# Another order inside the unit of attention: value products three units late, additions last

## The chip, the cores and the metric

The kernel runs on one core of a Trainium2 chip. The metric is the time of one execution in microseconds (us), as the device measures it; the median of several runs is compared. The engines are named as in the profile: PE (matrix products), PEld (its weight loads), DVE (vector), ACT (scalar and activation), POOL (GpSimd) and SP (which issues most DMA transfers).

## The reference

One layer of a decoder trunk, sequence 2048, width 1024, 16 query heads of 64 columns in two key/value groups, all in float32. The part that matters here is sliding-window attention with a sink:

```python
logits = jnp.einsum('bnqhgd,bnkhd->bnhgqk', qb, kb) * (HEAD_DIM ** -0.5) + bias
logits = jnp.where(mask, logits, NEG_INF)          # window of 128, blocks of 128
probs = jax.nn.softmax(jnp.concatenate([logits, sink], axis=-1), axis=-1)[..., :-1]
out = jnp.einsum('bnhgqk,bnkhd->bnqhgd', probs, vb)
...
a = attention * jax.nn.silu(a_gate);  a = a @ w_attn_proj
p = (GroupLinear(MultiScaleCausalPool(p_in)) * pool_scale) * silu(p_gate);  p = p @ w_pool_proj
y = (sigmoid(m_a) * a + sigmoid(m_p) * p) @ w_out * (1 + gate)
x = layer_norm(alpha * x + y)
```

## The kernel before, in words

The sequence is worked in two passes (s = 0 and 1) of 1024 positions. Each pass has a phase of gate products and a phase of attention; a last phase, the mixing, has the output products and the layer norm. Products in float32 are made of three products of a high and a low part (`mm3`): the high part is a rounded copy made on ACT, the low part (`low`) is the difference made on DVE or POOL.

`attention` is one loop of 69 units, written out in Python. The first 64 units (`N`) are pairs of heads by blocks of 128 queries: `j = n // 8` is the pair of heads, `t` the half of the pass and `b` the block in it. Within each engine the order is that in which the loop writes the instructions (the wrappers `pe`, `act`, `dve`, `pool`, `sp` keep program order); engines wait for each other by semaphores that the framework sets from the tiles that are written and read. A tile of a tag with `bufs=1` can be written anew only when every reader of its predecessor is done.

One block of queries passes through the loop over several units. Before the change these are, for the block of unit n:

- unit n: four score products into a bank `lg` (`score_mms`); on DVE two fused additions of the bias with a running minimum ("maxima", `tensor_tensor_reduce`, shown as CUSTOM_DVE_ANT_0); on ACT two exponentials with their sums.
- unit n + 1: the reciprocal of the sums on DVE; the first head's probabilities are normalised on ACT, the second head's on DVE (`tensor_scalar`).
- unit n + 2: four transposes into the bank `pt` (`turn_mms`); a high part `pth` (ACT) and a low part `ptl` (DVE) of them; and at the end of the unit four value products into the bank `pv` (`value_mms`).
- unit n + 3: half of `pv` is copied to `o2` (ACT), and two additions on DVE put the sum of both halves into `o`.

So a unit of the loop writes work of four blocks. Beside it each unit has half of a projection of 24 products of 128x512 (`parts[i]`, twelve products in a unit), whose weights come from HBM. What the projection has made is taken up by further steps behind the unit's own work: `take_q` in units 6 and 0 of every eight (two ACT copies and two DVE instructions, for the queries of the next pair of heads), `pool_sums` and `pool_diff` for the pooling branch (POOL and DVE), `finish`, in which POOL multiplies `o` or the pooled values by their gates, and high and low parts of weights. The value bank `pv`, the bank `pt`, and the tiles `pth` and `ptl` have one buffer each; `lg` has two and `L` three:

```python
        return ps.tile([P, CH], F32, tag=tag, bufs={"mm": 4, "lg": 2, "pt": 1, "pv": 1}[tag], name=tag)
```

Of the kernel before, what the change touches and what calls it, by code (L numbers as in the profile page):

```python
# [12 lines left out]
F32 = mybir.dt.float32  # L13
F32R = mybir.dt.float32r
AF = mybir.ActivationFunctionType
ALU = mybir.AluOpType
# [3 lines left out]
P = 128  # L20
# [3 lines left out]
CH = 512  # L24
NCH = S // CH
NB = CH // P
HEADS = 16
HD = 64
# [31 lines left out]
def kernel(  # L60
# [70 lines left out]
    def low(engine, dst, src, hi):  # L131
        engine.tensor_tensor(dst, src, as32(hi), ALU.subtract)  # L132
# [617 lines left out]
    def attention(ph, s, q0, nxt):  # L750
# [4 lines left out]
        def ld(name, src):  # L755
            x = tp.tile([P, CH], F32, tag="ld", bufs=3, name=name)
            nc.sync.dma_start(x, src)
            return x
# [83 lines left out]
        def score_mms(j, b, q, qs):  # L842
            k0 = P if s == 0 and b == 0 else 0
            lg = bank("lg").rearrange("p (h k) -> p h k", h=2)
            for h in range(2):
                for hl in range(2):
                    mm(
                        lg[:, h, k0:],
                        qs[:, h, q * P : (q + 1) * P],
                        kk[:, j // 4, hl, b * P + k0 : (b + 2) * P],  # L850
                        start=hl == 0,
                        stop=hl == 1,
                    )
            return lg, k0

        def turn_mms(L, k0):
            pt = ps.tile([P, 2, 2, P], F32, tag="pt", bufs=1, name="pt")
            for hf in range(k0 // P, 2):
                for h in range(2):
                    pe.transpose(pt[:, hf, h, :], L[:, h, hf * P : (hf + 1) * P], ident)  # L860
            return pt
# [20 lines left out]
        bts = {0: bias_tile(0)}  # L882
        tiles = {0: fetch(*slots[0][:2])}
        parts, accs, sums = {}, {}, {}
        lgs, exps, Ls, pvs, outs, ags, pgs = {}, {}, {}, {}, {}, {}, {}
        opened = []
        act.activation(warm, mhalf, AF.Exp)

# [32 lines left out]
        for n in range(N + 5):  # L921
            j, t, b = n // U, n // NB % 2, n % NB
            if n < N:
                lgs[n] = score_mms(j, n % U, b, qs[j, t])
            pt = None
            if n - 2 in Ls:
                L, k0 = Ls.pop(n - 2)
                pt = turn_mms(L, k0)
            if n - 1 in exps:
                sm = exps[n - 1][2]  # L930
                dve.reciprocal(sm, sm)
            if n - 3 in pvs:
                pv = pvs.pop(n - 3)
                jj, tt, bb = (n - 3) // U, (n - 3) // NB % 2, (n - 3) % NB
                if bb == 0:
                    outs[jj, tt] = tp.tile([P, CH], F32, tag="o", bufs=2, name="o")
                if bb == 1:
                    ags[jj, tt] = ld("ag", gates_d["ag"][s, jj, tt])
                o2 = tp.tile([HD, 2, P], F32, tag="o2", bufs=2, name="o2")
                act.copy(o2, pv[HD:])  # L940
                for h in range(2):
                    dve.tensor_tensor(
                        outs[jj, tt][h * HD : (h + 1) * HD, bb * P : (bb + 1) * P], pv[0:HD, h, :], o2[:, h, :], ALU.add
                    )
            if n - 1 in exps:
                E, e0, sm = exps[n - 1]
                act.activation(E[:, 0, e0:256], E[:, 0, e0:256], AF.Copy, scale=sm[:, 0:1])
            if pt is not None:
                h0 = k0 // P
                pth = tp.tile([P, 2, 2, P], F32R, tag="pth", bufs=1, name="pth")  # L950
                ptl = tp.tile([P, 2, 2, P], F32R, tag="ptl", bufs=1, name="ptl")
                act.copy(pth[:, h0:], pt[:, h0:])
            if n < N:
                lg, c0 = lgs.pop(n)
                L = tp.tile([P, 2, 260], F32, tag="L", bufs=3, name="L")
                nm = tp.tile([P, 2], F32, tag="nm", bufs=4, name="nm")
                sm = tp.tile([P, 2], F32, tag="sm", bufs=4, name="sm")
                act.copy(L[:, :, 256], nsink[:, 2 * j : 2 * j + 2])
                for h in range(2):
                    dve.tensor_tensor_reduce(  # L960
                        L[:, h, c0:256],
                        lg[:, h, c0:],
                        bts[j][:, h, c0:],
                        1.0,
                        nsink[:, 2 * j + h : 2 * j + h + 1],
                        ALU.add,
                        ALU.min,
                        nm[:, h : h + 1],
                    )
                    act.activation(  # L970
                        L[:, h, c0:257],
                        L[:, h, c0:257],
                        AF.Exp,
                        bias=nm[:, h : h + 1],
                        scale=-1.0,
                        accum_out=sm[:, h : h + 1],
                    )
                exps[n] = (L, c0, sm)
            if pt is not None:
                low(dve, ptl[:, h0:], pt[:, h0:], pth[:, h0:])  # L980
            if n - 1 in exps:
                E, e0, sm = exps.pop(n - 1)
                dve.tensor_scalar(E[:, 1, e0:256], E[:, 1, e0:256], sm[:, 1:2], None, ALU.mult)
                Ls[n - 1] = (E, e0)
            i = n // 2
            if i < len(slots):
                kind, m, st = slots[i]
                if n % 2 == 0:
                    accs[kind, m, st], parts[i] = projection(us[st])
                parts[i](tiles[i // 2][1:], 4 * (n % 2), 4 * (n % 2) + 4)  # L990
            elif n >= 60:
                fill_one(n)
            if pt is not None:
                pvs[n - 2] = value_mms((n - 2) // U, (n - 2) % U, k0, pth, ptl)


            w = n // 4 + 1
            if n % 4 == 0 and 2 * w < len(slots):
                tiles[w] = fetch(*slots[2 * w][:2])
            if w in tiles and tiles[w][0] is not None:  # L1000
                raw, hi, lo = tiles[w]
                if n % 4 == 1:
                    act.copy(by_two(hi), raw)
                if n % 4 == 2:
                    low(pool, by_two(lo), raw, by_two(hi))
            if n % U == 2 and j + 1 < KT:
                bts[j + 1] = bias_tile(j + 1)
            for st in range(2):
                if n % U == 6 + 2 * st - (U if st else 0) and (m := j + 1 - st) < KT and ("q", m, st) in accs:
                    qs[m, st] = take_q(accs.pop(("q", m, st)))  # L1010
            for what in puts:
                put(pool if n >= 64 else sp, *what)
            puts.clear()
            for at, x, which in ((57, 0, 0), (60, 1, 0), (62, 0, 1), (64, 1, 1)):
                if n == at:
                    early_hi(x, which)
                if n == at + 1:
                    early_lo(x, which)
            if n in (59, 62):
                nxt_group[n // 62].mid()  # L1020
            if n == 64:
                opened[0].append(nxt_group[0].w[:, 0, :])
                act.copy(opened[0][4], opened[0][0])
            for st in range(2):
                if n % U == 3 + 2 * st and (j, st) in sums:
                    pgs[j, st] = ld("pg", gates_d["pg"][s, j, st])
                if n % U == ((4, 6 + (j + 1 < KT))[st]) and (j, st) in sums:
                    pl = pool_diff(j, sums.pop((j, st)), accs.pop(("mix", j, st)))
                    finish("p", pin_d[s], j, st, pl, pgs.pop((j, st)))
            for st in range(2):  # L1030
                if n % U == 2 + 2 * st and ("mix", j, st) in accs:
                    sums[j, st] = pool_sums(j, st, accs["mix", j, st])
            for x in [x for x in outs if n == x[0] * U + x[1] * NB + NB + 2]:
                finish("a", ain_d[s], *x, outs.pop(x), ags.pop(x))

            if n in (26, 42):
                fill_set("T1", n // 42, nxt_store["T1"], sp)
            for start, name in ((57, "B11"), (58, "B21"), (59, "T2"), (61, "B22")):
                if n == start:
                    for half in range(2):  # L1040
                        fill_set(name, half, nxt_store[name], sp)
            if n == 51:
                for q in nxt_group:
                    q.load(ph, False)
# [467 lines left out]
```

## Time and profile before

| | |
|---|---|
| median of 3 runs | 1761.59 us (1759.8 to 1762.62) |
| the profiled execution | 1766.1 us, span in the profile 1763.9 us |
| mean granted PE clock | 0.991 |
| busy: PE, PEld | 1702.4 us (97%), 1427.4 us (81%) |
| busy: DVE, ACT, POOL | 1206.9 us (68%), 934.1 us (53%), 794.2 us (45%) |
| the two passes of attention | about 417 to 690 us and 1018 to 1290 us of the span |

How to read the rows: the timeline has start and length in us, engine, line, operation, and `out<-in` by the names of the tiles, then the shapes; `x4` stands for so many instructions in a row, and in brackets stands how long the engine was idle before and what ended that. A row of a stretch has its length and then, for each engine, the busy time and the instructions, then the granted clock, the share of the DMA engines and GB/s. A row of waits has the total, the times and the longest. A row of a tile has the shortest, median and longest duration in ns. Nearly all instructions of the loop have the line of a wrapper, L56, so they are told apart by their tiles.

### The profile page before, as it was taken

How to read it: one execution, taken by the hardware profiler on the slowest of the kernel's cores; microseconds unless marked ns; L12 is line 12 of the kernel's file. 1: busy time of each engine (PE TensorE's matmuls, PEld its weight loads, DVE VectorE, ACT ScalarE, POOL GpSimd, SP SyncE). 2: the span in 40 equal slices, each digit the busy share in tenths (PEclk: the TensorE clock that was granted, in tenths of full speed). 3: DMA queues.
4: the chain of work that ended last, by engine and by line, in shares of the span. 5: the costliest groups of instructions: out<-in, count | busy, mean ns of one | idle time of the engine just before them, and what ended most of it. 6: DMA issues, size and time to landing. Idle time of an engine off the chain costs nothing. (4 is left out here: it accounts for less than half of the span.)

```text
span 1763.9 us, 24990 instructions
## 1 busy us (share of the span) xinstructions
PE 1702.4 (97%) x8248; PEld 1427.4 (81%) x8248; DVE 1206.9 (68%) x2178; ACT 934.1 (53%) x1973; POOL 794.2 (45%) x618
## 2 busy tenths in 40 slices
PE   6899999999999998999999999999999989999997
PEld 5688888878888887888788888888888867888785
DVE  5977665655777776766655367777867676764777
ACT  4644444545777775544444377777734343423452
POOL 2154444431356567534434125456763562364542
PEclk9999999999999999999999999999999999999998
DMA  9385767844354567787777634544796675789442
GB/s 364 117 289 174 269 208 270 273 145 132 108 174 147 171 217 288 249 288 253 258 264 261 232 96 135 177 159 141 265 349 215 197 256 169 240 302 386 162 143 108
DMA packets 180466, 381.30 MB, mean 216 GB/s; under 512 B 18785, under 2 KB 39281, under 8 KB 180337
## 3 DMA queue, kind: packets, MB, share of 16 engines
q1 hardware_dynamic: 173696, 363.92, 60.5%
q0 software_dynamic: 3552, 11.56, 1.7%
q10 hardware_dynamic: 3088, 4.23, 0.8%
q8 instruction: 65, 1.06, 0.3%
q14 instruction: 65, 0.52, 0.1%
HBM read 244.35 MB, written 138.44 MB: 217 GB/s over the span
## 5 line engine op out<-in xcount | busy, mean ns | idle before, releaser
L56 PE MATMUL mm<-set_B,w_set 128*128 128x512 f32 x3240 | 798.7, 395 | 14.5 <-ACT u L376 6.3
L56 PEld LDWEIGHTS mm<-set_B,w_set 128*128 128x128 f32 x3240 | 603.3, 189 | 142.6 <-DVE w_set L132 10.3
L56 PE MATMUL lg<-set_T,w_set 128*128 128x512 f32 x2088 | 509.1, 394 | 18.4 <-DVE w_set L132 11.0
L56 PEld LDWEIGHTS lg<-set_T,w_set 128*128 128x128 f32 x2088 | 391.4, 189 | 111.0 <-DVE w_set L132 17.9
L132 DVE TENSOR_TENSOR w_set<-W,w_set 128x1024 fp32r<-128x1024 f32 x162 | 227.9, 1407 | 185.8 <-ACT w_set L325 180.8
L325 ACT CAST w_set<-W 128x1024 fp32r<-128x1024 f32 x162 | 169.8, 1049 | 251.6 <-PE mm L56 190.3
L56 PE MATMUL mm<-set_T,w_set 128*128 128x512 f32 x1080 | 265.5, 394 | 0.0
L56 PEld LDWEIGHTS mm<-set_T,w_set 128*128 128x128 f32 x1080 | 200.5, 188 | 41.0
L294 POOL TENSOR_TENSOR W<-W,A 128x512 f32<-128x512 f32 x56 | 82.1, 1466 | 227.6 <-DMA W<-in_win_dram 63.6
L303 POOL TENSOR_TENSOR W<-W 128x512 f32<-128x512 f32 x56 | 80.5, 1438 | 174.5 <-DVE w_set L132 165.2
L56 DVE TENSOR_TENSOR o<-pv,o 64x128 f32<-64x128 f32 x256 | 72.3, 283 | 89.8 <-ACT o L56 86.9
L56 ACT ACTIVATE L<-L,nm 128x257 f32<-128x257 f32 (+1 forms) x256 | 127.1, 498 | 9.3 <-DVE nm L56 3.9
L298 POOL TENSOR_TENSOR W<-W 128x512 f32<-128x512 f32 x56 | 90.5, 1618 | 84.7 <-DVE w_set L132 75.6
L56 DVE CUSTOM_DVE_ANT_0 L<-lg,bt,nsink 128x256 f32<-128x256 f32 (+1 forms) x256 | 111.6, 473 | 5.0 <-PE lg L56 0.8
L299 POOL TENSOR_TENSOR W<-W 128x512 f32<-128x512 f32 x56 | 84.7, 1513 | 37.9 <-DMA W<-in_win_dram 21.9
L56 POOL TENSOR_TENSOR w_set<-W,w_set 128x1024 fp32r<-128x1024 f32 x14 | 33.7, 2404 | 139.6 <-ACT w_set L56 96.9
L56 POOL TENSOR_TENSOR p<-nxt,pg 128x512 f32<-128x512 f32 x32 | 41.7, 1302 | 105.5 <-DVE sm L56 101.8
L56 ACT COPY o<-pv 64x256 f32<-64x256 f32 x128 | 47.3, 370 | 78.0 <-PE pv L56 77.2
L56 DVE TENSOR_TENSOR ptl<-pt,pth 128x512 fp32r<-128x512 f32 (+1 forms) x128 | 85.7, 669 | 1.9 <-ACT pth L56 1.7
L56 PE MATMUL lg<-kk,qs 128*128 128x256 f32 (+1 forms) x512 | 80.5, 279 | 0.0
L56 ACT ACTIVATE L<-L,sm 128x256 f32<-128x256 f32 (+1 forms) x128 | 64.2, 502 | 29.8 <-DVE sm L56 29.8
L56 ACT CAST pth<-pt 128x512 fp32r<-128x512 f32 (+1 forms) x128 | 73.5, 574 | 10.3
(212 smaller groups left out, 2296.3 us busy)
## 6 DMA issues: line engine op xcount, KB each, us to landing
W<-in_win_dram SPq DMA_DIRECT2D x48, 512.0 KB, 5.5
w_set<-wmix_d SPq DMA_DIRECT2D x32, 512.0 KB, 5.4
W<-in_win_dram SPq DMA_DIRECT2D x34, 256.0 KB, 3.7
A<-in_win_dram SPq DMA_DIRECT2D x34, 256.0 KB, 5.1
ag_d<-sig SPq DMA_DIRECT2D x32, 256.0 KB, 3.8
pg_d<-sig SPq DMA_DIRECT2D x32, 256.0 KB, 4.0
ma_d<-sig SPq DMA_DIRECT2D x32, 256.0 KB, 4.0
mp_d<-sig SPq DMA_DIRECT2D x32, 256.0 KB, 4.0
```

The source lines that it names most:

```text
L56: return lambda *args, **kw: self.tc.keep_in_program_order(op(*args, **kw))
L132: engine.tensor_tensor(dst, src, as32(hi), ALU.subtract)
L294: e.tensor_tensor(self.w[:, 1, :], self.w[:, 2, :], self.a22, ALU.add)
L298: e.tensor_tensor(x[:, 1, :], x[:, 1, :], x[:, 0, :], ALU.subtract)
L299: e.tensor_tensor(x[:, 2, :], x[:, 0, :], x[:, 2, :], ALU.subtract)
L303: e.tensor_tensor(x[:, 3, :], x[:, 3, :], x[:, 1, :], ALU.subtract)
L325: a.copy(by_two(hi), raw)
```

## The change

The value products of a block move from the end of unit n + 2 to unit n + 3, behind the scores of that unit and ahead of its transposes. `pth` and `ptl` are kept for that in `turned`. The projection is written directly behind the transposes. On ACT the copy of the sinks and the first normalising come first, then the copies of `pv` and `pt`, then the exponentials. On DVE the order is: reciprocal, the two maxima, the low part, the second normalising, and at last the two additions (before: reciprocal, additions, maxima, low part, normalising). The load of the attention gate (`ld("ag")`) is issued with the additions.

```diff
-                lgs[n] = score_mms(j, n % U, b, qs[j, t])
-            pt = None
+                lg, c0 = score_mms(j, n % U, b, qs[j, t])
+            pt = pv = None
+            if n - 3 in turned:
+                pv = value_mms((n - 3) // U, (n - 3) % U, *turned.pop(n - 3))
             if n - 2 in Ls:
                 L, k0 = Ls.pop(n - 2)
-                pt = turn_mms(L, k0)
+                pt, h0 = turn_mms(L, k0), k0 // P
+            i = n // 2
+            if i < len(slots):
...
+                parts[i](tiles[i // 2][1:], 4 * (n % 2), 4 * (n % 2) + 4)
+            elif n >= 60:
+                fill_one(n)
+            if n < N:
...
+                act.copy(L[:, :, 256], nsink[:, 2 * j : 2 * j + 2])
             if n - 1 in exps:
-                sm = exps[n - 1][2]
-                dve.reciprocal(sm, sm)
-            if n - 3 in pvs:
...
+                E, e0, r = exps[n - 1]
+                dve.reciprocal(r, r)
+                act.activation(E[:, 0, e0:256], E[:, 0, e0:256], AF.Copy, scale=r[:, 0:1])
+            if pv is not None:
                 o2 = tp.tile([HD, 2, P], F32, tag="o2", bufs=2, name="o2")
                 act.copy(o2, pv[HD:])
-                for h in range(2):
-                    dve.tensor_tensor(
-                        outs[jj, tt][h * HD : (h + 1) * HD, bb * P : (bb + 1) * P], pv[0:HD, h, :], o2[:, h, :], ALU.add
-                    )
...
             if pt is not None:
                 low(dve, ptl[:, h0:], pt[:, h0:], pth[:, h0:])
+                turned[n - 2] = k0, pth, ptl
             if n - 1 in exps:
-                E, e0, sm = exps.pop(n - 1)
-                dve.tensor_scalar(E[:, 1, e0:256], E[:, 1, e0:256], sm[:, 1:2], None, ALU.mult)
+                E, e0, r = exps.pop(n - 1)
+                dve.tensor_scalar(E[:, 1, e0:256], E[:, 1, e0:256], r[:, 1:2], None, ALU.mult)
                 Ls[n - 1] = (E, e0)
...
-            if pt is not None:
-                pvs[n - 2] = value_mms((n - 2) // U, (n - 2) % U, k0, pth, ptl)
+            if pv is not None:
+                jj, tt, bb = (n - 3) // U, (n - 3) // NB % 2, (n - 3) % NB
+                if bb == 0:
+                    outs[jj, tt] = tp.tile([P, CH], F32, tag="o", bufs=2, name="o")
+                if bb == 1:
+                    ags[jj, tt] = ld("ag", gates_d["ag"][s, jj, tt])
+                for h in range(2):
+                    dve.tensor_tensor(
+                        outs[jj, tt][h * HD : (h + 1) * HD, bb * P : (bb + 1) * P], pv[0:HD, h, :], o2[:, h, :], ALU.add
+                    )
```

More of the change, by code (lines that the diff above doesn't have):

```diff
@@ L884, in attention @@
         parts, accs, sums = {}, {}, {}
-        lgs, exps, Ls, pvs, outs, ags, pgs = {}, {}, {}, {}, {}, {}, {}
+        exps, Ls, turned, outs, ags, pgs = {}, {}, {}, {}, {}, {}
         opened = []
@@ L932, in attention @@
-            if n - 3 in pvs:
[L933 to L938, printed above, removed]
+                pt, h0 = turn_mms(L, k0), k0 // P
+            i = n // 2
+            if i < len(slots):
+                kind, m, st = slots[i]
+                if n % 2 == 0:
+                    accs[kind, m, st], parts[i] = projection(us[st])
+                parts[i](tiles[i // 2][1:], 4 * (n % 2), 4 * (n % 2) + 4)
+            elif n >= 60:
+                fill_one(n)
@@ new lines, in attention @@
+            if n < N:
+                L = tp.tile([P, 2, 260], F32, tag="L", bufs=3, name="L")
+                nm = tp.tile([P, 2], F32, tag="nm", bufs=4, name="nm")
+                sm = tp.tile([P, 2], F32, tag="sm", bufs=4, name="sm")
+                act.copy(L[:, :, 256], nsink[:, 2 * j : 2 * j + 2])
+            if n - 1 in exps:
+                E, e0, r = exps[n - 1]
+                dve.reciprocal(r, r)
+                act.activation(E[:, 0, e0:256], E[:, 0, e0:256], AF.Copy, scale=r[:, 0:1])
@@ L939, in attention @@
+            if pv is not None:
                 o2 = tp.tile([HD, 2, P], F32, tag="o2", bufs=2, name="o2")
                 act.copy(o2, pv[HD:])
-                for h in range(2):
-                    dve.tensor_tensor(
-                        outs[jj, tt][h * HD : (h + 1) * HD, bb * P : (bb + 1) * P], pv[0:HD, h, :], o2[:, h, :], ALU.add
-                    )
-            if n - 1 in exps:
-                E, e0, sm = exps[n - 1]
-                act.activation(E[:, 0, e0:256], E[:, 0, e0:256], AF.Copy, scale=sm[:, 0:1])
@@ L948, in attention @@
             if pt is not None:
-                h0 = k0 // P
                 pth = tp.tile([P, 2, 2, P], F32R, tag="pth", bufs=1, name="pth")
@@ L953, in attention @@
             if n < N:
[L954 to L958, printed above, removed]
                 for h in range(2):
@@ L980, in attention @@
                 low(dve, ptl[:, h0:], pt[:, h0:], pth[:, h0:])
+                turned[n - 2] = k0, pth, ptl
             if n - 1 in exps:
-                E, e0, sm = exps.pop(n - 1)
-                dve.tensor_scalar(E[:, 1, e0:256], E[:, 1, e0:256], sm[:, 1:2], None, ALU.mult)
+                E, e0, r = exps.pop(n - 1)
+                dve.tensor_scalar(E[:, 1, e0:256], E[:, 1, e0:256], r[:, 1:2], None, ALU.mult)
                 Ls[n - 1] = (E, e0)
[L985 to L992, printed above, removed]
-            if pt is not None:
-                pvs[n - 2] = value_mms((n - 2) // U, (n - 2) % U, k0, pth, ptl)
+            if pv is not None:
[8 more added lines that the diff above has]
+                    )
             w = n // 4 + 1
```

## The prediction

> **What bounds the kernel now.** I read the page's busy times first, then the stretches by engine, then the waits of PE, then the timeline of some units of the attention loop, and last the tiles that the change touches.
>
> ```profile
> span 1763.9 us, 24990 instructions
> PE 1702.4 (97%) x8248; PEld 1427.4 (81%) x8248; DVE 1206.9 (68%) x2178; ACT 934.1 (53%) x1973; POOL 794.2 (45%) x618
> ...
> 500.00:560.00 60.00, 60.00 (x347) 52.73 (x347) 45.51 (x142) 45.47 (x138) 28.61 (x23) 1.00 0.51 161
> ...
> 1140.00:1200.00 60.00, 60.00 (x349) 52.75 (x348) 43.23 (x139) 44.99 (x133) 30.38 (x24) 1.00 0.45 149
> ...
> PE mm L56 <- ACT u L376: 6.3, 1, 6.3
> ```
>
> PE bounds the program, and inside both passes of attention it is busy all the time: 60.00 of 60 us, at a granted clock of 1.00. The reader is to see that an order of instructions can win almost nothing there, because DVE and ACT already hide behind PE. One idle piece stands near attention: 6.3 us at its end, behind a chain of ACT and DVE work of the next stage.
>
> The timeline of two units (DVE, ACT, PE rows; start, length, engine) gives every duration that I need:
>
> ```profile
> 501.90 0.37 ACT L56 COPY o<-pv 64x256 f32<-64x256 f32 x1 [0.68 <-PE pv L56]
> ...
> 502.17 0.51 ACT L56 ACTIVATE L<-L,sm 128x256 f32<-128x256 f32 x1
> ...
> 502.53 3.02 PE L56 MATMUL mm<-set_B,w_set 128*128 128x512 f32 x12
> ...
> 505.38 0.28 PE L56 MATMUL pv<-pth,vv 128*128 128x256 f32 x1
> ...
> 505.76 0.54 PEld L56 LDWEIGHTS lg<-kk,qs 128*128 128x128 f32 x4
> 505.88 0.63 PE L56 MATMUL lg<-kk,qs 128*128 128x256 f32 x4
> ...
> 506.35 0.60 PE L56 MATMUL pt<-ident,L 128*128 128x128 f32 x4
> ...
> 506.70 3.00 PE L56 MATMUL mm<-set_T,w_set 128*128 128x512 f32 x12
> 506.98 0.59 ACT L56 CAST pth<-pt 128x512 fp32r<-128x512 f32 x1
> ...
> 507.46 0.20 ACT L56 COPY L<-nsink 128x2 f32<-128x2 f32 x1
> ...
> 507.69 0.51 ACT L56 ACTIVATE L<-L,nm 128x257 f32<-128x257 f32 x1
> ...
> 508.20 0.50 ACT L56 ACTIVATE L<-L,nm 128x257 f32<-128x257 f32 x1
> ...
> 508.69 1.18 ACT L56 ACTIVATE qs<-mm 64x512 fp32r<-64x512 f32 x2
> ...
> 509.91 1.39 DVE L56 SCALAR_TENSOR_TENSOR qs<-mm,qs 64x512 fp32r<-64x512 f32 x2 [1.06 <-ACT qs L56]
> ...
> 511.31 0.17 DVE L56 RECIPROCAL sm<-sm 128x2 f32<-128x2 f32 x1
> 511.51 0.58 DVE L56 TENSOR_TENSOR o<-pv,o 64x128 f32<-64x128 f32 x2
> 511.57 0.51 ACT L56 ACTIVATE L<-L,sm 128x256 f32<-128x256 f32 x1 [0.98 <-DVE sm L56]
> 512.11 0.59 ACT L56 CAST pth<-pt 128x512 fp32r<-128x512 f32 x1
> 512.12 0.49 DVE L56 CUSTOM_DVE_ANT_0 L<-lg,bt,nsink 128x256 f32<-128x256 f32 x1
> ...
> 512.94 0.69 DVE L56 TENSOR_TENSOR ptl<-pt,pth 128x512 fp32r<-128x512 f32 x1
> ...
> 513.54 0.35 DVE L56 TENSOR_SCALAR L<-L,sm 128x256 f32<-128x256 f32 x1
> 513.71 0.28 PE L56 MATMUL pv<-pth,vv 128*128 128x256 f32 x1
> ...
> 513.80 0.68 DVE L56 SCALAR_TENSOR_TENSOR nxt<-nxt,mm 128x512 f32<-128x512 f32 x1
> ...
> 514.40 0.16 DVE L56 RECIPROCAL sm<-sm 128x2 f32<-128x2 f32 x1
> ```
>
> **The change part by part.** I count from the start of a unit's projection ("P") and call the other PE groups S (scores), T (transposes) and V (value products). From the rows: P to P 4.17 us (502.53 to 506.70), P to what follows it 2.85 (502.53 to 505.38), V 0.50, S 0.47, T 0.35. Nothing is removed or added on any engine.
>
> *PE.* Before, the cycle is S T P V; after, S V T P. So only S and V swap places behind P: S starts at 2.85, V at 3.32 instead of 2.85. The sum of the pitches is the same: 0.
>
> *DVE and ACT.* The two additions that read the value bank move from the front of the unit to its end, behind the low part and the second normalising. The copy of the sinks and the first normalising move ahead of the copy of pv on ACT. Maxima come earlier by up to 0.58.
>
> *The added wait.* The value bank (tag pv) is single. Before, V of a unit found it free long ago, since the additions stood at the front of the same unit. Now V of the next unit waits until the additions at the end of this one have been made. T and the twelve matmuls of P are queued behind V on PE, and all later units behind those, so every late addition is paid in full. Where is the slack? PE issues V's first weight load at the start of S's last matmul, 0.12 ahead (505.76 against 505.88): additions must be done by 3.32 - 0.12 = 3.20.
>
> A plain unit: copy of pt at 0.28 (506.70 to 506.98), low part 0.62 later (next fence), normalising 0.60 later (512.94 to 513.54), additions 0.26 later (513.54 to 513.80), 0.58 long, 0.06 to PE (653.47 + 0.69 to 654.22, next fence): 2.40. That is 0.80 early, and costs nothing.
>
> Not so in the unit after take_q, whose two DVE instructions wait for ACT and end late. Take_q stands in units 6 and 0 of each eight.
>
> - Unit 6: copy of pt 0.28, exponentials 0.48 later (507.46: the sinks' copy is out of the way now), 0.51 and 0.49 to qs, 1.22 to DVE's qs, 1.40 to the reciprocal (511.31): 4.38, which is 0.21 in unit 7.
> - Unit 7: normalising on ACT +0.26, copy of pv +0.54 (511.57 to 512.11), copy of pt +0.27 (501.90 to 502.17), low part +0.62, normalising +0.60, additions +0.26, their end +0.58, to PE +0.06: 3.19 after the reciprocal, 3.40. PE wanted it at 3.20: **0.20 late**. (Before, V needed only the low part: 512.94 + 0.69 = 513.63, against 513.71 for V. So this chain is already 0.08 from the edge.)
> - Unit 0: the additions start at 2.76, the pool difference 0.61 later (511.51 to 512.12), the reciprocal 0.60 after that (513.80 to 514.40): 3.97, less 4.17 + 0.20, is -0.40. The copy of pt comes 1.07 later at 0.67, and take_q follows: 0.67 + 0.48 + 0.51 + 0.49 + 1.22 + 1.40 = 4.77, or 0.60 in unit 1.
> - Unit 1: 0.60 + 3.19 = 3.79 against 3.20: **0.59 late**. Unit 2 starts without a backlog.
>
> ```profile
> L56 ACT ACTIVATE qs<-mm x64: 574/593/597, 413.0 to 1252.9; 64x512 fp32r<-64x512 f32 x64
> L56 DVE TENSOR_SCALAR L<-L,sm x128: 275/403/1452, 422.8 to 1285.0; 128x256 f32<-128x256 f32 x120, 128x128 f32<-128x128 f32 x8
> ...
> 633.87 0.69 DVE L56 SCALAR_TENSOR_TENSOR nxt<-nxt,mm 128x512 f32<-128x512 f32 x1 [1.49 <-POOL nxt L56]
> ...
> 637.62 0.96 PE L56 MATMUL pt<-ident,L 128*128 128x128 f32 x4
> ...
> 645.18 1.30 DVE L56 TENSOR_SCALAR L<-L,sm 128x256 f32<-128x256 f32 x1
> ...
> 646.22 0.86 PE L56 MATMUL pt<-ident,L 128*128 128x128 f32 x4
> ...
> 653.47 0.69 DVE L56 TENSOR_TENSOR ptl<-pt,pth 128x512 fp32r<-128x512 f32 x1
> ...
> 653.83 0.28 PE L56 MATMUL pv<-pth,vv 128*128 128x256 f32 x1
> ...
> 654.22 0.39 PE L56 MATMUL pv<-ptl,vv 128*128 128x256 f32 x1
> ...
> 680.20 0.59 ACT L56 CAST pth<-pt 128x512 fp32r<-128x512 f32 x1
> ...
> 680.82 0.69 DVE L56 TENSOR_TENSOR ptl<-pt,pth 128x512 fp32r<-128x512 f32 x1 [0.45 <-ACT pth L56]
> ```
>
> Each take_q has two ACT rows: 64 rows are 32 of them, of which four stand ahead of the loops. So 28 are in the loops, 14 pairs. 14 x (0.20 + 0.59) = 11.1 us. In the first pass the normalising of unit 1 is half as wide (0.28 instead of 0.35), 7 x 0.07: 10.6 us.
>
> *The second normalising's own length.* It runs 0.275 to 1.452 us, the long ones beside POOL. In a plain unit it must pass 0.35 + 0.80 = 1.15 before anything is late, so at most 0.30 is lost there. In the units after take_q all of its excess counts: 28 x (1.452 - 0.35) = 31 us at the far end, 0 at the near one. I take 2: of those 28 rows one is long (645.18: 1.30, nearly 1 us over), and about as much again for rows that shift into a POOL instruction.
>
> The Trainium skill, "SBUF — State Buffer", section "Who interferes with whom", says that tensor_scalar can enter a mode which takes the port pair shared with GpSimd, and that whoever comes second is blocked for the whole instruction. The spread of this one form agrees; no run here yet shows the effect at the new place.
>
> *What goes away.* PE now loses a little late in the first pass. The transposes at 637.62 and 646.22 take 0.96 and 0.86 instead of 0.60, because normalising comes late, and the second value product at 654.22 begins 0.39 behind the first instead of 0.12 (a quarter of V's 0.50), because the low part does. Normalising and the low part now come ahead of the additions: -(0.36 + 0.26 + 0.27) = -0.9.
>
> *Moved transfers.* The load of the gate ("ag") is issued in the same unit, still ahead of the unit's weight fetches on SP; 0. POOL's product of o and the gate waits for the additions, some 2 us later than before, with later pool sums behind it. Early in a pass POOL idles there. If that cover is gone, DVE waits for POOL as at 633.87 (1.49 us); in the last two blocks of both passes that would be 4 x 1.5 = 6. I take 0 and keep 6 for the top of the range.
>
> **Sum.** 10.6 + 2.0 - 0.9 = +11.7 us. The profiled execution took 1766.1 us (span 1763.9), so it would become 1777.8. The median of the runs is 1761.59, 4.5 lower; from it, 1773.
>
> **The rivals.** A change of less than 0.2% (3.5 us) can't be told from none here.
>
> *No change: the chain is shorter than I add up.* Each late addition is a sum of eight handovers; were they 0.07 shorter each, the 0.59 would vanish (0.07 x 8). It would also hold if V did not have to wait for the additions. Against it: the same chain puts V 0.08 behind the low part in the rows above, and the bank has one buffer. Time: 1761.6 - 0.9 to 1765.
>
> *Faster: the small stalls go and the end of attention shortens.* The 6.3 us of PE idle end with a chain of ACT and DVE work; if the reordered last units free ACT earlier, up to 6.3 + 0.9 = 7.2 are won: 1754. It decides if that chain starts over 2.6 us earlier with no stall in the units. Against it: in the last units PE's order (T, fill, V, fill) is the same as before.
>
> *Much slower: normalising is blocked by POOL after most take_q.* POOL is busy 28.61 of 60 us. Were every second one of the 28 to wait a whole POOL instruction (1.1), +15 comes on top: 1788; all of them, 1803. For it: the form's lengths up to 1.452. Against it: one of the 28 is long now. The rule of the Trainium skill named above (same page and section: the order of issue decides who blocks) speaks for this case, as the normalising is issued at another time.
>
> **How the numbers follow.** Forecast (slower by 4 to 22 us) 0.73; no change 0.11; faster 0.04; much slower 0.12. The likeliest time is 1773. For the range, a near end with only the 0.59 stalls, each 0.2 smaller, is 14 x 0.39 - 0.9 = +4.6, or half of that where handovers are shorter still: 1764; the far end adds POOL's 6 to the sum, and 5 for a sixth of the 28 normalisings blocked for a whole instruction: 1773 + 11 = 1784. Outside lie most of no change, the faster case and most of the much slower one: about 0.2.
>
> **What would show it.** In the changed profile PE should show waits "pv <- DVE o" of some 0.2 and 0.6 us, 28 or somewhat more, only in units 0 and 2 of each eight, and PE's busy share in 500 to 560 should fall from 60.00 to about 58.5. Plain units should stay at 4.17. The wait of 6.3 us at the end of the first pass should stay. The transposes' rows of 0.96 should be gone. Wrong would be: no wait of PE on o; waits of over 1 us in many units (then POOL's lock or POOL's lateness is the bound); or a change of that 6.3.

## Result and the profile after

The changed kernel takes 1777.24 us (median; 1775.18 to 1777.95), the kernel before 1762.11 us beside it: ratio 1.0084, 95% interval 1.0067 to 1.0101. It is slower by 15 us. The prediction said 1773, 1764 to 1784.

The page of the changed kernel, its waits of PE (total, times, longest), and two stretches:

```profile
span 1775.8 us, 24988 instructions
PE 1709.3 (96%) x8248; PEld 1429.3 (80%) x8248; DVE 1204.1 (68%) x2178; ACT 926.0 (52%) x1973; POOL 802.1 (45%) x618
...
PE pv L56 <- DVE o L56: 6.9, 15, 0.9
...
PE mm L56 <- ACT u L376: 5.3, 1, 5.3
...
500.00:560.00 60.00, 59.67 (x338) 51.72 (x337) 45.76 (x140) 44.12 (x137) 28.20 (x23) 1.00 0.51 162
1140.00:1200.00 60.00, 59.46 (x342) 51.79 (x341) 43.96 (x137) 42.69 (x129) 29.61 (x24) 1.00 0.49 161
```

A wait that no page of before had is there: value products wait for `o`, that is, for the additions. The row shows 15 waits and 6.9 us only, and the stretches are still nearly full, because a wait of 0.2 us lies under the modelled end of the product ahead of it (below, the scores of 1088.75 end by their row at 1089.38, and the value products behind them start at 1089.43). The instructions tell more: `x338` where `x347` stood in the same 60 us. I therefore measured from the starts of PE's rows. The table has the time between the first projection (or fill) products of units 0, 8, 52, 60, 66 and the first product behind the loop:

```
us from unit to unit        0-8    8-52   52-60  60-66  66-next  sum
pass 1  before             31.26  180.08  33.89  23.19   9.20   277.62
        after              31.50  183.17  34.39  25.84   8.17   283.07
pass 2  before             31.75  183.35  33.33  23.21   2.75   274.39
        after              31.97  187.96  34.36  25.67   2.75   282.71
```

Attention alone is longer by 5.5 + 8.3 = 13.8 us: 9.7 in units 0 to 60, 5.1 at the ends of the passes, and 1.0 less in the idle piece behind the first pass. The spans of the two profiles differ by 11.9; the rest of the program was 2 us shorter in this one execution.

By groups of PE (each from its start to the start of the next), units 0 to 60 of both passes have 10.5 us more from the scores to the value products, 0.7 less in the transposes and 0.1 less in all the rest. Of the value products in units 3 to 63, 34 start over 0.1 us late: the 28 in units 0 and 2 of every eight from unit 8 on, unit 12 and unit 54 of the first pass, and units 60 and 63 of both.

One pair of take_q in the second pass of the changed kernel, in the timeline (rows of PE, DVE and ACT; weight loads and other rows are left out):

```profile
1088.71 0.57 DVE L56 TENSOR_TENSOR o<-pv,o 64x128 f32<-64x128 f32 x2
...
1089.43 0.36 PE L56 MATMUL pv<-pth,vv 128*128 128x256 f32 x1
...
1092.52 1.19 ACT L56 ACTIVATE qs<-mm 64x512 fp32r<-64x512 f32 x2
1092.82 0.57 DVE L56 TENSOR_TENSOR o<-pv,o 64x128 f32<-64x128 f32 x2
1093.18 0.64 PE L56 MATMUL lg<-kk,qs 128*128 128x256 f32 x4
1093.65 0.28 PE L56 MATMUL pv<-pth,vv 128*128 128x256 f32 x1
...
1093.74 1.39 DVE L56 SCALAR_TENSOR_TENSOR qs<-mm,qs 64x512 fp32r<-64x512 f32 x2 [0.35 <-ACT qs L56]
1093.77 0.28 PE L56 MATMUL pv<-ptl,vv 128*128 128x256 f32 x1
...
1094.13 0.60 PE L56 MATMUL pt<-ident,L 128*128 128x128 f32 x4
...
1094.49 2.99 PE L56 MATMUL mm<-set_B,w_set 128*128 128x512 f32 x12
1095.15 0.17 DVE L56 RECIPROCAL sm<-sm 128x2 f32<-128x2 f32 x1
...
1097.32 0.63 PE L56 MATMUL lg<-kk,qs 128*128 128x256 f32 x4
1097.43 0.35 DVE L56 TENSOR_SCALAR L<-L,sm 128x256 f32<-128x256 f32 x1
...
1097.69 0.57 DVE L56 TENSOR_TENSOR o<-pv,o 64x128 f32<-64x128 f32 x2
...
1098.41 0.36 PE L56 MATMUL pv<-pth,vv 128*128 128x256 f32 x1 [0.46 <-DVE o L56]
1098.60 0.28 PE L56 MATMUL pv<-ptl,vv 128*128 128x256 f32 x1
```

Additions end at 1089.28, and V, the group of value products, starts at 1089.43; with scores at 1088.75 (0.47 long) it was due at 1089.22: 0.21 late. In the next unit V is on time. In the one after, with the reciprocal 0.66 behind the projection, the additions end at 1098.26 and V, due at 1097.32 + 0.47 = 1097.79, starts at 1098.41: 0.62 late.

### The profile page after: what moved, and what is told of

Its sections match the earlier page's. It is cut to its first block, busy times and chain, and to the rows that moved or that the text cites. A ratio compares the mean times of both kernels' runs of the same rounds, so it can differ in the third digit from the quotient of the medians.

```text
span 1775.8 us, 24988 instructions
## 1 busy us (share of the span) xinstructions
PE 1709.3 (96%) x8248; PEld 1429.3 (80%) x8248; DVE 1204.1 (68%) x2178; ACT 926.0 (52%) x1973; POOL 802.1 (45%) x618
## 5 line engine op out<-in xcount | busy, mean ns | idle before, releaser
L294 POOL TENSOR_TENSOR W<-W,A 128x512 f32<-128x512 f32 x56 | 87.3, 1560 | 216.3 <-DMA W<-in_win_dram 48.5
L56 PEld LDWEIGHTS lg<-kk,qs 128*128 128x128 f32 x512 | 78.2, 189 | 9.9
L56 DVE TENSOR_TENSOR k_lo<-spare,k_hi 128x512 fp32r<-128x512 f32 x61 | 61.0, 1003 | 27.2 <-ACT k_hi L56 9.0
```

What stands on the lines that cost most here:

```text
L56: return lambda *args, **kw: self.tc.keep_in_program_order(op(*args, **kw))
L294: e.tensor_tensor(self.w[:, 1, :], self.w[:, 2, :], self.a22, ALU.add)
```

## The experiments

Each run is compared with the kernel before on the same chip, as a ratio. The chips of the three groups had medians of 1765.75, 1766.26 and 1763.95 us for it.

**Two value banks up to block 51.** The theory is that the single bank, freed by additions that are now last, is the cost; the rival, that late value products or ACT's order cost by themselves.

```diff
-            pv = bank("pv")[:, 0 : 2 * P]...
+            m = j * U + b
+            pv = bank("mm" if m % 2 and m < 52 else "pv")[:, 0 : 2 * P]...
```

> The changed kernel, but the value products of every odd block up to block 51 of a pass go into a fourth bank of the projections' tag, so that in the loop they need not wait for the additions of the block before; the last twelve blocks keep the one bank. Theory A (the single value bank, freed only by additions that are now last on DVE, is the whole cost): PE's waits on o vanish up to unit 55, 12 of the 14 pairs of about 0.8 us with them; what is left is the last pair of each pass and the units behind the loop, together about 6 us; 1762 - 1 + 6 = 1767. Rival B (value products three units late, or the new order on ACT, costs by itself): the waits move to other tiles (pth, ptl, L) and the time stays at 1777.

Measured: 1.0026 (1.0015 to 1.0038), +4.6 us. From unit 8 to 52 the passes take 179.54 and 182.80 us, 0.5 less than before, against 3.1 and 4.6 more with one bank. The waits that are left stand where the bank is single again:

```profile
PE pv L56 <- DVE o L56: 5.9, 9, 1.2
```

So in units 8 to 52 the bank is the whole cost, and the value products' new place costs nothing.

**Additions first.**

```diff
                 act.copy(o2, pv[HD:])
+                # the two additions here, ahead of the maxima
...
-                # and no longer behind the second normalising
```

> The changed kernel with the two additions back at the front of the unit on DVE, ahead of the maxima; value products stay three units late and ACT's new order stays. Theory A: additions are made more than 2 us before the next value products, no wait of PE on o; as before or 1 us less: 1761 to 1763. Rival B (the later value products or ACT's order cost by themselves): 1777, or at least 1770.

Measured: 1.0262 (1.0240 to 1.0285), +46 us. Theory A missed by far. Rival B's bound (at least 1770) holds, but not its size of 1777: the waits on `o` are gone, and larger ones on `ptl` have come. The waits of PE, and the unit after a take_q:

```profile
PE pv L56 <- DVE ptl L56: 26.7, 34, 1.1
...
1151.59 0.17 DVE L56 RECIPROCAL sm<-sm 128x2 f32<-128x2 f32 x1
1151.85 0.51 ACT L56 ACTIVATE L<-L,sm 128x256 f32<-128x256 f32 x1 [1.48 <-DVE sm L56]
1152.26 0.35 ACT L56 COPY o<-pv 64x256 f32<-64x256 f32 x1
...
1152.65 0.58 DVE L56 TENSOR_TENSOR o<-pv,o 64x128 f32<-64x128 f32 x2 [0.90 <-ACT o L56]
...
1153.26 0.48 DVE L56 CUSTOM_DVE_ANT_0 L<-lg,bt,nsink 128x256 f32<-128x256 f32 x1
...
1154.08 0.69 DVE L56 TENSOR_TENSOR ptl<-pt,pth 128x512 fp32r<-128x512 f32 x1
...
1154.82 0.39 PE L56 MATMUL pv<-ptl,vv 128*128 128x256 f32 x1 [1.08 <-DVE ptl L56]
```

ACT's new order has the normalising ahead of the copy of pv. So DVE hands the reciprocal to ACT and then stands idle 0.90 us for a copy that could have been made long ago; maxima, exponentials and low part queue behind the additions. Theory D: it is ACT's order that makes additions first dear, not the late value products.

**Value products three units late, and nothing else.**

```diff
+            if n - 3 in pvs:                       # behind the scores
+                pvs[n - 3] = value_mms((n - 3) // U, (n - 3) % U, *pvs[n - 3])
...
-            if pt is not None:                     # at the end of the unit
-                pvs[n - 2] = value_mms((n - 2) // U, (n - 2) % U, k0, pth, ptl)
```

> The kernel before with one edit: the value products of a block move behind the scores of the next unit (three units late); DVE and ACT keep their old order (copy of pv ahead of the first normalising, additions ahead of the maxima). Against the earlier run with additions first, only ACT's order differs. Theory D, from that run: what makes additions first so dear (+46) is that ACT makes the copy of pv only behind the first normalising, which waits for the reciprocal; additions, maxima, exponentials and low part all queue behind it. Then this kernel is as before, 0 to -1. Rival: value products that come later make the additions and all behind them late by themselves; then +10 or more.

> The value products three units late alone, once more with five rounds, to see whether this version is faster than the kernel before. By its profile the passes of attention are 1.4 and 0.7 us shorter than before: ratio 0.9988; faster by more than 0.2% is not expected.

Measured: 0.9988 (0.9974 to 1.0002), and again 0.9992 (0.9982 to 1.0002). Sums of the passes: 276.20 and 273.67, that is 1.4 and 0.7 less than before. Theory D stands: only ACT's order differs from the run with additions first, and 46 us with it. That this version is faster than the kernel before is likely and not shown.

**Additions last, and nothing else.** The kernel before with the two additions behind the second normalising.

> The kernel before with one edit: the two additions go behind the second normalising on DVE; value products stay at the end of the unit and ACT keeps its old order. Theory A (PE waits for the one value bank until late additions are made): the bank is wanted at 2.62 after the start of the projection (2.85 less a weight load) instead of 3.20; plain units are ready at 2.40, so 0.2 is left; units after take_q are ready at 3.4, 0.75 late, twice in eight units: 14 x 1.5 = 21, and normalising that waits for POOL by more than 0.2 adds some 5 to 15: 25 to 35 over before. Rival B (it is the three units or ACT's order that cost): as before.

Measured: 1790.29 us in a single run, 24 more than the median before. The passes take 289.91 and 288.71 us, +26.6 together; 25 to 35 was named for theory A. The waits of PE:

```profile
PE pv L56 <- DVE o L56: 15.9, 40, 0.6
```

So the additions' place costs more with value products at the end of the unit, and the rest of the change gave back half of it. A run below, with the copy of pv in its old place on ACT, has passes of 284.61 and 283.79 us, +16.4: by these profiles moving the value products gave back some 10 us, and ACT's order some 3.

**Additions ahead of the second normalising**, behind the low part, in the changed kernel.

> The changed kernel with the two additions one place earlier on DVE, ahead of the second normalising. Theory A with the chain as it was added up: additions end 0.34 us earlier (or more where normalising waited beside POOL), so the wait of 0.20 in unit 0 goes and that of 0.6 in unit 2 falls to about 0.25; the transposes get normalised values 0.58 later, as before the change. 14 x 0.25 + 2 = about +4 to +6 over before: 1767. Rival C (POOL's blocking of normalising is what makes additions late): all waits go but those without POOL; 1763.

Measured: 1.0077 (1.0060 to 1.0093), no gain. The wait of 0.2 in unit 0 is gone in 11 of the 14 pairs, as forecast. The one in unit 2 is 0.6 to 0.8 late in the second pass and 0.3 or 0.65 in the first, not 0.25. A new wait of the transposes for the second normalising, and the same pair in its timeline:

```profile
PE pt L56 <- DVE L L56: 1.8, 8, 0.6
...
1096.60 3.95 POOL L56 TENSOR_TENSOR p<-p,p 128x512 f32<-128x512 f32 x3
...
1098.02 1.38 DVE L56 TENSOR_SCALAR L<-L,sm 128x256 f32<-128x256 f32 x1
...
1099.43 1.39 DVE L56 SCALAR_TENSOR_TENSOR qs<-mm,qs 64x512 fp32r<-64x512 f32 x2
...
1103.84 0.36 PE L56 MATMUL pv<-pth,vv 128*128 128x256 f32 x1 [0.60 <-DVE o L56]
```

In this pair, and in the others of units 16, 32 and 48, normalising starts just behind the start of one of POOL's three products and ends just behind that product's end (1.38 us instead of 0.35). Take_q starts late behind it, so the backlog of the next unit is larger, and V in unit 2 is 0.77 to 0.79 late in the second pass. In the other four pairs of that pass no normalising is long, and V is still 0.6 late. In three of these PE didn't wait in unit 0, so unit 1 began sooner against the same work of DVE: in the first pair its reciprocal stands 0.92 behind the projection instead of 0.66, which eats most of the 0.34. And what the value products still won in the second pass between units 0 and 60 (1.1 us), the transposes lost (1.2).

**The copy of pv ahead of the first normalising** on ACT, in the changed kernel.

> The changed kernel with ACT's copy of pv back ahead of the first normalising; the additions stay last. Theory A with the chain as added up: the copy of pv (0.27) leaves the chain from the reciprocal to the copy of pt, so additions end 0.27 earlier where a unit starts late: 0.20 falls to 0, 0.6 to 0.3; 14 x 0.3 + 3 at the ends of the passes, about 1768. If ACT's order were the whole cost (rival B): 1762. If it plays no part: 1777.

Measured: 1.0090 (1.0074 to 1.0106), no gain either. A unit with take_q:

```profile
1049.33 0.37 ACT L56 COPY o<-pv 64x256 f32<-64x256 f32 x1 [1.67 <-PE pv L56]
1049.48 3.02 PE L56 MATMUL mm<-set_T,w_set 128*128 128x512 f32 x12
1049.60 0.51 ACT L56 ACTIVATE L<-L,sm 128x256 f32<-128x256 f32 x1
1050.13 0.59 ACT L56 CAST pth<-pt 128x512 fp32r<-128x512 f32 x1
```

The 0.27 was saved where units start late, but in all units ACT now waits for V before it normalises. The copy of pt comes 0.65 behind the start of the projection instead of 0.28, take_q 0.37 later, and the pair has two waits of 0.3 instead of 0.2 and 0.6 in the second pass. Plain units wait too: 40 value groups start late instead of 34.

**Two banks to the end of the pass.** The same with "mm" up to block 55 and "lg" for blocks 57 to 61.

> The changed kernel with a second bank for the value products of every odd block to the end of each pass (from the projections' banks, the last three from the scores' banks). Theory A: no wait of PE on o anywhere; the first run with two banks kept about 5 us over before, from the last pair of take_q and the end of each pass, and that goes too: before, or up to 2 us less, since the small stalls on the transposes are gone and the wait at the end of the first pass is 5.3 instead of 6.3. If the ends of the passes have another cause: +3 to +5 stays.

Measured: 1.0039 (1.0024 to 1.0053); before or less was expected. No wait on `o` is left, but units 52 to 60 and 60 to 66 still take 1.6 + 3.3 and 1.0 + 3.6 us more than before. Other waits have come there that the kernel before doesn't have:

```profile
PE mm L56 <- DVE nxt L56: 1.3, 2, 0.7
PE mm L56 <- DVE w_set L56: 0.8, 2, 0.5
```

In the first row a product waits for the pool difference, which reads a bank of the projections' tag, so probably a borrowed bank is missed. In the second, products wait for a low part of weights. The rows make up only a part of the 9.5 us, so what the ends lose here is not shown in full, and the run doesn't tell what they cost with their own banks; the next one does.

**Additions ahead of the low part from unit 62 on.**

> The changed kernel with the additions ahead of the low part again in the units from 62 on alone, where no maxima are left. Theory A for the ends of the passes: additions stand there behind the low part and the normalising, and behind weights' low parts that DVE makes in units 61 and 63; the waits of 0.6 to 1.0 us in the last four units fall to 0.2 or less: 2 x 1.5 to 2 = 3 to 4 us less than the changed kernel, +10 to +12 over before. If those waits come from the copy of pv that ACT makes late: 0.

Measured: 1.0073 (1.0050 to 1.0096). Units 60 to 66 take 23.95 and 23.74 us instead of 25.84 and 25.67; before had 23.19 and 23.21. So of the 5.1 us at the ends, 3.8 are the additions' place. Not all of it is won: the stretch from unit 66 to the first product behind the loop takes 8.67 and 3.31 us instead of 8.17 and 2.75, 1.1 more. The ratio alone wouldn't show any of this; the stretches do.

**The second take_q two units later** (unit 2 of eight instead of 0).

> The changed kernel with the second take_q of each pair two units later (unit 2 of eight instead of unit 0), so that the backlog of the first is worked off before it. The prediction's chain (a backlog that grows from 0.20 to 0.59 over the pair): each take_q then starts from a unit without backlog and costs the 0.20 of the first, in units 0 and 4; no wait of 0.6 is left in the second pass; 14 x 0.2 to 0.4 = 3 to 5 us less than the changed kernel. If each take_q costs by itself, wherever it stands (no backlog carried over): two waits of about 0.4 in place of 0.2 and 0.6, and the same time.

Measured: 1.0125 (1.0105 to 1.0144), slower still. In the second pass the wait of 0.2 in unit 0 stays and unit 2 has none, as the backlog wants it. But the moved take_q doesn't cost 0.2: in the same pass V in unit 4 is 0.3 to 1.0 late, and 0.6 to 1.25 in the first pass. In the rows below it is 0.48 (scores at 1115.17, V due at 1115.64). There normalising runs beside POOL's product of `o` and its gate (1114.03, 1.30 long) and takes 0.54 instead of 0.35. That product stands behind POOL's sums, which start later too, since take_q stands ahead of their copies on ACT. It explains a part of the 0.48.

```profile
1114.95 0.54 DVE L56 TENSOR_SCALAR L<-L,sm 128x256 f32<-128x256 f32 x1
...
1116.12 0.36 PE L56 MATMUL pv<-pth,vv 128*128 128x256 f32 x1 [0.32 <-DVE o L56]
```

Near the end of each pass V in unit 4 waits longest, 2.67 us by its row in the first. The run confirms that the 0.6 is a backlog of two take_q, and refutes the price that I gave the moved one.

## Why the prediction was right, and where not

*The wait.* Right in place and kind. Two banks took the loop's waits away; additions last alone brought them with no other edit.

*0.20 and 0.59 per pair.* In the second pass 0.21 and 0.62, in the order of units forecast. In the first pass the second one was mis-sized: V at 515.3 and 523.9 starts 0.41 and 0.32 behind the last score product, 0.29 and 0.20 late. I took 0.07 off for a narrower normalising; but in block 0 of a pair all rows are narrower, here in the kernel before:

```profile
648.43 0.41 ACT L56 ACTIVATE L<-L,nm 128x129 f32<-128x129 f32 x1
...
648.84 0.39 ACT L56 ACTIVATE L<-L,nm 128x129 f32<-128x129 f32 x1
```

Two exponentials 0.1 shorter each start take_q 0.2 earlier, and maxima and scores shrink too. Of the forecast 10.6 + 2.0 - 0.9 = 11.7 us for the loop, 9.7 came (units 0 to 60): 10.5 of waits instead of 12.6, and 0.8 won instead of 0.9.

*2 us for normalising beside POOL.* Wrong in place; that the size is near is luck. The 2 us stood for the 28 rows in units behind a take_q, and in the changed kernel none of these is over 0.35 us. The waits came in plain units, which the prediction let lose 0.30 at most: V in units 12, 54 and 60 of the first pass is 0.19, 0.65 and 0.34 late, and in unit 60 of the second 0.17, 1.35 us together. In the unit ahead of each the normalising is long (1.08 to 1.34 us). Unit 53, for which unit 54 pays, had moreover 1.01 us in which DVE waited for POOL's sums, as it had in the kernel before (1.49). Its normalising and the wait behind it, and the same for the longest normalising, in unit 62:

```profile
638.88 1.16 DVE L56 TENSOR_SCALAR L<-L,sm 128x256 f32<-128x256 f32 x1
...
640.68 0.36 PE L56 MATMUL pv<-pth,vv 128*128 128x256 f32 x1 [0.49 <-DVE o L56]
...
677.51 1.29 POOL L298 TENSOR_TENSOR W<-W 128x512 f32<-128x512 f32 x1
677.51 1.43 DVE L56 TENSOR_SCALAR L<-L,sm 128x256 f32<-128x256 f32 x1
...
679.59 0.36 PE L56 MATMUL pv<-pth,vv 128*128 128x256 f32 x1 [0.85 <-DVE o L56]
```

In unit 62 DVE's instruction starts with POOL's and ends 0.14 behind it, after 1.43 us instead of 0.35. That agrees with the rule of the Trainium skill, "SBUF — State Buffer", section "Who interferes with whom", that the one who comes second is blocked for the whole instruction. The rival built on it (every second take_q blocked, 1788) did not come, since none of these rows is lengthened in the changed kernel; in the two runs that moved normalising or take_q such rows are part of the loss.

*0 at the ends of the passes.* Wrong: +5.1. I looked at PE's order, which is the same, and not at DVE's. There stand low parts of weights (1.77 us) ahead of the reciprocal, ACT's copies wait for that, and the additions come last. In unit 62 such a low part (1.48 us) and the normalising of 1.43 us come together, and V in unit 63 is 1.0 and 0.8 us late in the two passes. The last wait of the first pass, in its rows:

```profile
683.57 1.77 DVE L56 TENSOR_TENSOR w_set<-W,w_set 128x1024 fp32r<-128x1024 f32 x1
...
685.26 0.16 DVE L56 RECIPROCAL sm<-sm 128x2 f32<-128x2 f32 x1
685.45 0.51 ACT L56 ACTIVATE L<-L,sm 128x256 f32<-128x256 f32 x1 [2.68 <-DVE sm L56]
...
687.87 0.57 DVE L56 TENSOR_TENSOR o<-pv,o 64x128 f32<-64x128 f32 x2
688.58 0.36 PE L56 MATMUL pv<-pth,vv 128*128 128x256 f32 x1 [0.63 <-DVE o L56]
```

In all the passes cost 13.8 us instead of the 11.7 forecast: 5.1 more at the ends, 2.0 less in the loop, and 1.0 less in the idle piece behind the first pass. So the nearness of 1773 to 1777 is in part luck, as misses of both signs cancel. The last 1.3 of the 15.1 us between the medians lie in no stretch of the table; the ratio's interval is wider than that.

*The idle piece of 6.3 us.* It was to stay, and a change of it was named as a sign of being wrong; it is 5.3. Probably a part of it is now waited out ahead of it, in the last units: with additions early from unit 62 on, where these waits shrink, its longest wait is 5.8. No run isolates that.

*What would show it.* Of the 34 late value groups 28 stand in units 0 and 2, as forecast, and 6 do not. The lengthened transposes of before are gone, and plain units keep their pitch. Busy PE of 58.5 in 500 to 560 was wrong (59.67): short waits don't show as idle time, as said above.

## What to carry to other kernels

Before moving a reader of a single-buffered tile to the end of its engine's queue, add up the chain from the latest start of that queue to the tile's next writer; where the writer's engine is the bound, each late reader is paid in full. A stall also gives the other engines time: without it the next unit starts sooner against the same work of theirs. And shortening one link (0.34 or 0.27 us here) won nothing, because the same move made another later: the transposes in one run, ACT's copies in the other. An instruction that moves on one engine can make a harmless order on another dear: additions first cost nothing with the old order on ACT, and 46 us with the new one.

## What the runs showed that was not expected

A wait of PE costs more than its length. After it, the second value product starts 0.19 behind the first (1098.41 to 1098.60) instead of 0.12 (1093.65 to 1093.77). The load of its weights, in the rows of PE's weight loads of the changed kernel, begins 0.07 behind the first product, and 0.01 where there was no wait:

```profile
1093.66 0.19 PEld L56 LDWEIGHTS pv<-ptl,vv 128*128 128x128 f32 x1
...
1098.48 0.19 PEld L56 LDWEIGHTS pv<-ptl,vv 128*128 128x128 f32 x1
```

Over some 35 waits in the two passes that is an estimated 2.5 us, which the prediction did not have.

A smaller gain stands against it. A value group that waits for nothing takes 0.48 us from its start to the transposes behind it (1093.65 to 1094.13; median 0.479), and 0.495 in the kernel before, where it stands behind the projection. Over 126 groups that is an estimated 2 us. In the run with the value products three units late alone, it is nearly all that units 0 to 60 of the second pass win (1.0 us); why the group is shorter there is not shown.
